# A hybrid encoder layer on one core: the order of weight pairs in the input chunks, six pairs in five output chunks, and some work moved by a step or more

## The chip, the core and the metric

The kernel runs on one core of a Trainium2 chip. Its engines are TensorE (PE; its weight loads are a row of their own, PEld), VectorE (DVE), ScalarE (ACT), GpSimd (POOL) and SyncE (SP, which issues nearly all DMAs). The metric is the time on the device in microseconds: 1500.56 us is the median of three runs (1500.46 to 1501.62).

## The reference

All in float32, with 256 tokens and a width of 4096. The factors that the matrices have are left out here.

```python
h = layer_norm(x, emb_ln_g, emb_ln_b)
p = h @ w_in                                  # 256 x 4096 @ 4096 x 13312: c_b, c_c, c_h, c_z, a_q, a_k, a_v, a_z
y_conv = c_b * conv3_centred(c_c * c_h, conv_w) * silu(c_z)
y_attn = banded_window_attention(a_q, a_k, a_v, sink) * silu(a_z)   # 16 heads of 128, 4 kv heads, window 128, ALiBi, sink
y = concatenate([y_conv, y_attn]) @ w_out     # 256 x 4096 @ 4096 x 4096
out = layer_norm(2 ** 0.25 * h + y, ln_g, ln_b)
```

## The kernel before

**Products.** Both projections are done in three products of a rounded type: each operand is split into a high half (rounded) and a low half (the rest), and hi x hi, lo x hi and hi x lo are summed. The activations lie in `xT`, transposed, hi and lo. The weights are streamed: each piece is loaded from memory as float32, ScalarE writes its high half (`split_hi`, tile `whi`, L226), VectorE subtracts for its low half (`split_lo`, tile `wlo`, L230), and TensorE reads both. There are three buffers of `whi` and three of `wlo`, so the splitting runs at most three steps ahead.

**Chunks and steps.** The input projection is cut into 26 chunks of 512 columns (two for k and v, then for each of four groups a gate z and a q, then for each of four groups cc, ch, cz, cb), the output projection into 9 (seven of 512 columns, two of 256). A chunk is a row of steps, written as a string. An "s" is a whole piece: 4 k-tiles by 512 columns, 1,024 KB, 48 matmuls of 256 columns. An "S" is a pair: 2 k-tiles, 512 KB, computed with seven block products in place of eight (a Strassen scheme), 21 matmuls. A pair needs sums of weight blocks (`sums`, on VectorE before the split) and sums of activation blocks, which are made once (`x_sums`, into `SC`; for the output projection `y_sums`, into `SCy`). Two pairs that follow each other are a couple: their sums are made in one go (L192 to L194 in place of L205 to L207 twice), and both must then lie in the four slots of the tile `wall`; a single pair or a piece can also be loaded into other places (`w6` to `w8`, or `R` in the output chunks).

**A step.** Step j does, in this order: the matmuls of step j, `split_hi(j + 3)`, whatever was booked for the step with `at`, the loads that have room (`loads`), `sums(j + 4)`, `split_lo(j + 3)`. Nothing else schedules: each engine works through its instructions in that order, SP through its DMAs, with semaphores between.

**Attention.** It runs beside the chunks, booked by `SPREAD`: after a q chunk each of the group's four heads gets a step for each of its parts: scores, s_add (L601), exps, recip, norms, p_tr (probabilities transposed, and their high half by ScalarE, L636), p_lo (their low half by VectorE, L641), pv (L648 and L650), out_z (L654, which also stores to `yd`). The transposes of z (L518) share a PSUM pool of two banks with them.

**Output chunks.** `residual` prepares alpha times the normed input from loaded rows (`gb`: two scale rows and ln_g; `xc`: x), `end_out` adds it and takes statistics, `end_out2` multiplies by ln_g. `rows_load` and `rows_split` prepare ln_g and ln_b as rows for the last norm: 15 small DMAs (L908).

Of the kernel before, what the change touches and what calls it, by code (L numbers as in the profile page):

```python
# [34 lines left out]
NPC = KT // PK  # L35
# [6 lines left out]
HT = S // 2  # L42
NP = 8
NP1 = 4
PAIRS = [0, 0, NP1] + [NP] * (len(IN_ORDER) - 3)
ORDERS = {0: "s" * 8, NP1: "sssSSsSsSs", NP: "sSSsSSSSsSSs"}
OUT = 100
OP = 4
OUT_ORDERS = ["s" * 8] * 2 + ["sSsSsSsSss"] * 5 + ["", ""]
N_W = 4  # L50
OFF = 4
GAP = 64
# [49 lines left out]
def encoder_kernel(ctx: ExitStack, tc: tile.TileContext, x, emb_g, emb_b, wi, ws, conv_w, sink, wo, ln_g, ln_b, out):  # L102
# [21 lines left out]
    def couple(j):  # L124
# [5 lines left out]
    psc = pw = pc = R = None  # L130
    extra = []
    user = {}
    in_R = [(steps.index(("opair", OUT + 4, OP - 1)) + 1, "R0"), (steps.index(("opair", OUT + 4, OP - 1)) + 1, "R1"),
            (steps.index(("opair", OUT + 6, OP - 1)) + 1, "R2")]

    def w_bufs(j):

# [520 lines left out]
    def head(n, *steps):  # L658
        return [(t, f, n) for t, f in zip(steps, (scores, s_add, exps, recip, norms, p_tr, p_lo, pv, out_z))]

    SPREAD = [(6, q_tr, 0), (7, q_lo, 0), (10, q_tr, 1), (11, q_lo, 1)] + head(0, 8, 9, 9, 10, 10, 13, 15, 19, 20) + head(
        1, 9, 10, 10, 11, 12, 19, 21, 22, 23) + head(2, 13, 17, 18, 19, 20, 24, 27, 28, 29) + head(
        3, 21, 22, 22, 23, 23, 28, 30, 31, 32)

    def open_pc():
        nonlocal pc
# [115 lines left out]
        for hi, lo, y in y_parts(q):  # L782
            nc.vector.tensor_tensor(lo, y, hi.bitcast(F32), op=ALU.subtract)

    X_SUMS = [NPC + 2 + k for k in range(NP1)] + [2 * NPC + k for k in (1, 4, 6, 8)]
    build_tab()
    later = {}

    def at(j, fn, *a):
        later.setdefault(j, []).append((fn, a))  # L790
# [76 lines left out]
    def bcast(src, a, n):  # L867
        return bass.AP(tensor=src.tensor, offset=src.offset + a, ap=[[0, P], [1, n]])
# [32 lines left out]
    def rows_split():  # L901
        for k, (slots_h, slot_l) in enumerate((((0, 1), 2), ((3,), 4))):
            w, hl = lnw[k], R[0:KT, k, 3 * W + P:3 * W + 3 * P].bitcast(F32R).rearrange("p (a b) -> p a b", a=2)
            nc.vector.tensor_copy(hl[:, 0, :], w)
            nc.vector.tensor_tensor(hl[:, 1, :], w, hl[:, 0, :].bitcast(F32), op=ALU.subtract)
            for b, a0, n in ((0, 0, 12), (32, 12, 12), (64, 24, 8)):
                for r, h in [(r, 0) for r in slots_h] + [(slot_l, 1)]:
                    nc.sync.dma_start(out=rows[b + r:b + r + 1, 0:n * P].bitcast(F32), in_=hl[a0:a0 + n, h, :].bitcast(F32))  # L908

    def res_load(n):  # L910
        if n >= ncs:
            return
        c0, w, _, _ = chunks[n]
        if n < ncs - 1:
            gb = p2.tile([P, 3, w], F32, name="gb")
        if n < ncs - 2:
            xc = p2.tile([P, 2, W], F32, name="xc")[:, :, 0:w]
        elif n == ncs - 2:
            xc = z_tile()[:, 6 * W:6 * W + 2 * w].rearrange("p (a b) -> p a b", a=2)
        else:  # L920
            z = zt[0]
            gb = z[:, 0:3 * w].rearrange("p (a b) -> p a b", a=3)
# [7 lines left out]
        nc.sync.dma_start(out=gb[:, 2, :], in_=bcast(ln_g, c0, w))  # L930
        for i in range(2):
            nc.sync.dma_start(out=xc[:, i, :], in_=x[i * P:(i + 1) * P, c0:c0 + w])
        res[n] = gb, xc

    def residual(n):
        gb, xc = res[n]
        for i in range(2):
            nc.vector.scalar_tensor_tensor(xc[:, i, :], xc[:, i, :], musd[:, i, 0:1], gb[:, 0, :],
                                           op0=ALU.subtract, op1=ALU.mult)
            nc.vector.scalar_tensor_tensor(xc[:, i, :], xc[:, i, :], musd[:, i, 2:3], gb[:, 1, :],  # L940
                                           op0=ALU.mult, op1=ALU.add)
# [34 lines left out]
        return r  # L976

    def end_out2(n, i, r):
        nc.vector.tensor_tensor(r, r, res[n][0][:, 2, :], op=ALU.mult)
# [189 lines left out]
```

## Time and profile before

| | |
|---|---|
| median of three runs | 1500.56 us |
| profiled execution | 1500.92 us, span 1499.2 us |
| granted TensorE clock, mean | 0.999 |
| TensorE busy | 1482.4 us (99%), 12,878 matmuls |
| VectorE, ScalarE busy | 1338.4 us (89%), 803.3 us (54%) |
| DMA | 316.17 MB, 211 GB/s over the span |
| per chunk of the input projection with eight pairs | 40.8 us (688.0 to 728.8) to 46.9 us (285.0 to 331.9) |
| per output chunk with four pairs | 42.1 to 42.2 us |

A row of a group reads: line, engine, operation, out<-in, shapes, count | busy us, mean ns of one | idle us of the engine before it and what ended that. A matmul's busy time overlaps the next one's, so what TensorE loses at a wait is read from the weight loads. A wait is put down to the engine whose signal the profile takes for the last.

### The profile page before, as it was taken

The numbers are of one execution on the slowest core, as the hardware profiler recorded it, in microseconds if no ns is written. First come the engines' busy times: TensorE is split into PE (matmuls) and PEld (weight loads), VectorE is DVE, ScalarE is ACT, GpSimd is POOL, SyncE is SP. The second block draws the span as 40 slices with busy tenths as digits, with TensorE's granted clock in tenths as the row PEclk, the third lists the DMA queues.
The fourth block names the chain that finished last, engine by engine and source line by source line (L and its number), as shares of the span: only waits on it lengthen the run. The fifth ranks groups of instructions, "written<-read, shape, count | busy, mean of one in ns | idle before, by whom it ended". The sixth has DMA issues, their size and how long they took to land.

```text
span 1499.2 us, 29810 instructions
## 1 busy us (share of the span) xinstructions
PE 1482.4 (99%) x12878; PEld 1465.4 (98%) x12878; DVE 1338.4 (89%) x1384; ACT 803.3 (54%) x687; POOL 1.3 (0%) x7
## 2 busy tenths in 40 slices
PE   7999999999999999999999999999999999999998
PEld 4999999999999999999999999999999999999997
DVE  7768999898999999999999999999998688888876
ACT  5544656766666665655555555555555444444431
POOL 0000000000000000000000000000000000000000
PEclk9999999999999999999999999999999999999999
DMA  8545465555554556646545655556558656756663
GB/s 318 217 183 196 164 217 189 192 197 208 180 204 176 190 201 209 230 177 224 200 182 219 231 198 197 225 204 241 191 207 313 233 201 220 290 215 230 219 237 113
DMA packets 71365, 316.17 MB, mean 211 GB/s; under 512 B 8545, under 2 KB 12609, under 8 KB 50113
## 3 DMA queue, kind: packets, MB, share of 16 engines
q1 hardware_dynamic: 70224, 312.43, 57.3%
q8 instruction: 101, 1.65, 0.4%
q10 hardware_dynamic: 1008, 1.84, 0.3%
q14 instruction: 32, 0.25, 0.0%
HBM read 305.23 MB, written 8.91 MB: 210 GB/s over the span
## 4 chain that ended last, share of the span: by engine, by line
PE 93%; DVE 3%; ACT 1%; issue 1%; DMA 1%; SPq 0%; ACTq 0%; DVEq 0%
PE acc L275 39%; PE acc L957 20%; PE pacc L301 6%; PE pacc L300 6%; PE pacc L303 6%; PE acc L301 4%; PE acc L300 4%; PE acc L303 4%; DVE wlo L230 1%; PE att L518 1%; ACT whi L226 1%; DVE st L354 0%; PE acc L404 0%; DMA wall<-in_ws 0%; DVE wall L192 0%
## 5 line engine op out<-in xcount | busy, mean ns | idle before, releaser
L226 ACT ACTIVATE whi<-wall 128x1792 fp32r<-128x1792 f32 (+1 forms) x284 | 501.7, 1772 | 464.6 <-DVE wall L194 149.7
L230 DVE TENSOR_TENSOR wlo<-wall,whi 128x1792 fp32r<-128x1792 f32 (+1 forms) x284 | 593.4, 2096 | 75.9 <-ACT whi L226 64.3
L275 PE MATMUL acc<-whi,xT 128*128 128x256 f32 x3584 | 427.6, 276 | 0.0
L275 PEld LDWEIGHTS acc<-whi,xT 128*128 128x128 f32 x3584 | 415.8, 188 | 0.0
L275 PE MATMUL acc<-wlo,xT 128*128 128x256 f32 x1792 | 221.3, 275 | 0.0
L275 PEld LDWEIGHTS acc<-wlo,xT 128*128 128x128 f32 x1792 | 211.4, 188 | 0.0
L226 ACT ACTIVATE whi<-w 128x2048 fp32r<-128x2048 f32 x73 | 140.7, 1927 | 114.6 <-PE acc L275 72.5
L957 PE MATMUL acc<-whi,xT 128*128 128x256 f32 x1696 | 201.8, 275 | 0.0
L957 PEld LDWEIGHTS acc<-whi,xT 128*128 128x128 f32 x1696 | 196.6, 188 | 0.4 <-issue 0.4
L230 DVE TENSOR_TENSOR wlo<-w,whi 128x2048 fp32r<-128x2048 f32 x73 | 166.8, 2286 | 10.8 <-ACT whi L226 10.6
L192 DVE TENSOR_TENSOR wall<-wall 128x1024 f32<-128x1024 f32 x93 | 113.3, 1218 | 11.0 <-DMA wall<-in_ws 8.7
L300 PE MATMUL acc<-whi,xT 128*128 128x256 f32 x416 | 114.7, 276 | 0.0
L301 PE MATMUL acc<-whi,xT 128*128 128x256 f32 x416 | 114.6, 276 | 0.0
L300 PE MATMUL pacc<-whi,xT 128*128 128x256 f32 x396 | 111.0, 280 | 0.0
L303 PE MATMUL pacc<-wlo,xT 128*128 128x256 f32 x396 | 109.2, 276 | 0.6 <-DVE wlo L230 0.4
L301 PE MATMUL pacc<-whi,xT 128*128 128x256 f32 x396 | 109.1, 276 | 0.0
L957 PE MATMUL acc<-wlo,xT 128*128 128x256 f32 x848 | 105.3, 275 | 0.0
L303 PE MATMUL acc<-wlo,xT 128*128 128x256 f32 x416 | 104.4, 275 | 0.0
L300 PE MATMUL pacc<-whi,SC 128*128 128x256 f32 x376 | 103.6, 275 | 0.0
L301 PE MATMUL pacc<-whi,SC 128*128 128x256 f32 x376 | 103.6, 275 | 0.0
L957 PEld LDWEIGHTS acc<-wlo,xT 128*128 128x128 f32 x848 | 100.4, 188 | 0.0
L303 PE MATMUL pacc<-wlo,SC 128*128 128x256 f32 x376 | 94.5, 276 | 0.0
(224 smaller groups left out, 1930.1 us busy)
## 6 DMA issues: line engine op xcount, KB each, us to landing
wall<-in_ws SPq DMA_DIRECT2D x202, 512.0 KB
w<-in_wi SPq DMA_DIRECT2D x73, 1024.0 KB
wall<-in_wo SPq DMA_DIRECT2D x43, 1024.0 KB
wall<-in_wi SPq DMA_DIRECT2D x39, 1024.0 KB
R<-in_wo SPq DMA_DIRECT2D x10, 1024.0 KB
x<-in_x SPq DMA_DIRECT2D x7, 512.0 KB
yl<-yd SPq DMA_DIRECT2D x7, 512.0 KB
xc<-in_x SPq DMA_DIRECT2D x14, 256.0 KB
```

What stands on the lines that cost most here:

```text
L192: nc.vector.tensor_tensor(t[:, :, 4:6, :], t[:, :, 1:3, :], t[:, :, 0:1, :].to_broadcast([P, 2, 2, HW]), op=ALU.add)
L226: nc.scalar.activation(part(j, wh[j]), part(j, raw[j]), AF.Copy)
L230: nc.vector.tensor_tensor(part(j, wl[j]), part(j, raw[j]), part(j, wh[j]).bitcast(F32), op=ALU.subtract)
L275: nc.tensor.matmul(acc[ci, i][:, c:c + HW], x, w[:, k * W + c:k * W + c + HW], start=(first and w is hi and k + off + c == 0), stop=(last ...
L300: nc.tensor.matmul(o, ah, hi[:, w, :], start=(opens and p == 0), stop=False)
L301: nc.tensor.matmul(o, al, hi[:, w, :], start=False, stop=False)
L303: nc.tensor.matmul(o, ah, lo[:, w, :], start=False, stop=(closes and last))
L518: nc.tensor.transpose(ps[:, c, i * P:(i + 1) * P], t[:, i, (2 * b + c) * P:(2 * b + c + 1) * P], ident)
L957: nc.tensor.matmul(acc[ci, i][:, c:c + HW], y, m[:, k * w + c:k * w + c + HW], start=(first and off + c == 0), stop=(last and c + HW == w))
```

## The change

- In the 23 input chunks with eight pairs the order goes from s SS s SSSS s SS s to s SSSS s SS s SS s.
- Output chunks 2 to 6 have six pairs and five pieces in place of four and six. The pairs stand in couples. Two more `y_sums` are made, and all six start three steps sooner, in output chunk 0.
- `p_lo` of the four heads stands one, one, two and one step sooner.
- The `x_sums` of pair 7 move from step 24, in the chunk before, to step 31, in the first chunk that needs them.
- ln_g gets a tile of its own with two buffers (`lg`), so `end_out2` can come three steps later; `residual` comes two steps later.
- `rows_load` and `rows_split` come a chunk sooner, and the 15 DMAs are booked two a step.

```diff
-ORDERS = {0: "s" * 8, NP1: "sssSSsSsSs", NP: "sSSsSSSSsSSs"}
+ORDERS = {0: "s" * 8, NP1: "sssSSsSsSs", NP: "sSSSSsSSsSSs"}
 OUT = 100
-OP = 4
-OUT_ORDERS = ["s" * 8] * 2 + ["sSsSsSsSss"] * 5 + ["", ""]
+OP = 6
+OUT_ORDERS = ["s" * 8] * 2 + ["sSSsSSsSSss"] * 5 + ["", ""]
...
-    SPREAD = [(6, q_tr, 0), (7, q_lo, 0), (10, q_tr, 1), (11, q_lo, 1)] + head(0, 8, 9, 9, 10, 10, 13, 15, 19, 20) + head(
-        1, 9, 10, 10, 11, 12, 19, 21, 22, 23) + head(2, 13, 17, 18, 19, 20, 24, 27, 28, 29) + head(
-        3, 21, 22, 22, 23, 23, 28, 30, 31, 32)
+    SPREAD = [(6, q_tr, 0), (7, q_lo, 0), (10, q_tr, 1), (11, q_lo, 1)] + head(0, 8, 9, 9, 10, 10, 13, 14, 19, 20) + head(
+        1, 9, 10, 10, 11, 12, 19, 20, 22, 23) + head(2, 13, 17, 18, 19, 20, 24, 25, 28, 29) + head(
+        3, 21, 22, 22, 23, 23, 28, 29, 31, 32)
...
-    X_SUMS = [NPC + 2 + k for k in range(NP1)] + [2 * NPC + k for k in (1, 4, 6, 8)]
+    X_SUMS = [NPC + 2 + k for k in range(NP1)] + [2 * NPC + k for k in (1, 4, 6, 15)]
...
-                    nc.sync.dma_start(out=rows[b + r:b + r + 1, 0:n * P].bitcast(F32), in_=hl[a0:a0 + n, h, :].bitcast(F32))
+                    row_moves.append((rows[b + r:b + r + 1, 0:n * P].bitcast(F32), hl[a0:a0 + n, h, :].bitcast(F32)))
+        for k, (o, i) in enumerate(row_moves):
+            at(j + 1 + k // 2, row_move, o, i)
...
-            gb = p2.tile([P, 3, w], F32, name="gb")
+            gb = p2.tile([P, 2, w], F32, name="gb")
+            lg = p2.tile([P, w], F32, name="lg", bufs=2)
...
     for k in range(OP):
-        at(chunks[1][3] + 1 + k, y_sums, k)
+        at(N_IN + 6 + k, y_sums, k)
...
-            if t == 0 and n:
+            if t == (3 if n < ncs - 2 else 0) and n:
                 for a in ends:
                     end_out2(*a)
                 ends = []
-                if n < ncs - 1:
-                    res_load(n)
-            if t == (0 if n == ncs - 1 else 2 if n == ncs - 2 else 4 if n else 7):
+            if t == 0 and 0 < n < ncs - 1:
+                res_load(n)
+            if t == (0 if n == ncs - 1 else 2 if n == ncs - 2 else 6 if n else 7):
                 residual(n)
-            if n == 2 and t == 4:
+            if n == 1 and t == 4:
                 rows_load()
-            if n == 2 and t == 8:
-                rows_split()
+            if n == 1 and t == 6:
+                rows_split(j)
```

Three places show what it does to the order.

VectorE, around the low half of the probabilities of a group's fourth head (`kp` is the tile that holds the probabilities, `wlo` the low halves of weights, `wall` rows are the sums of a couple, `zT` is `out_z` of the head before). Before:

```order
L230 TENSOR_TENSOR wlo0_3425<-wall_92,whi_3409 128x1792
L654 TENSOR_TENSOR zT_2019<-att_3411,zT_2019 128x256
L192 TENSOR_TENSOR wall_92<-wall_92 128x2x512
L193 TENSOR_TENSOR wall_92<-wall_92 128x2x256
L194 TENSOR_TENSOR wall_92<-wall_92 128x2x256
L230 TENSOR_TENSOR wlo1_3456<-w6_3299,whi_3448 128x2048
L641 TENSOR_TENSOR kp_645<-att_3418,kp_645 128x512
L230 TENSOR_TENSOR wlo2_3489<-wall_92,whi_3479 128x1792
```

After:

```order
L230 TENSOR_TENSOR wlo0_3399<-wall_92,whi_3381 128x1792
L654 TENSOR_TENSOR zT_2021<-att_3383,zT_2021 128x256
L641 TENSOR_TENSOR kp_645<-att_3390,kp_645 128x512
L192 TENSOR_TENSOR wall_92<-wall_92 128x2x512
L193 TENSOR_TENSOR wall_92<-wall_92 128x2x256
L194 TENSOR_TENSOR wall_92<-wall_92 128x2x256
L230 TENSOR_TENSOR wlo1_3458<-wall_92,whi_3449 128x2048
L230 TENSOR_TENSOR wlo2_3491<-wall_92,whi_3481 128x1792
```

The low half (L641) has moved ahead of a couple's sums and of the split of a whole piece.

SP, at the end of a q chunk in attention (`in_ws` is a pair's load, `in_wi` a piece's, `yd` the store of `out_z`, `kp<-kd` the reload of k). Before:

```order
L172 DMA wall_92<-in_ws 128x1024 x2
L172 DMA wall_92<-in_wi 128x2048 x2
L172 DMA wall_92<-in_ws 128x1024
L655 DMA yd0_72<-zT_2019 128x256
L172 DMA wall_92<-in_ws 128x1024
L172 DMA w6_3042<-in_wi 128x2048
L172 DMA wall_92<-in_ws 128x1024
L554 DMA kp_645<-kd_648 128x512
```

After:

```order
L172 DMA wall_92<-in_ws 128x1024 x2
L172 DMA w6_2848<-in_wi 128x2048
L172 DMA wall_92<-in_wi 128x2048
L172 DMA wall_92<-in_ws 128x1024 x2
L655 DMA yd0_72<-zT_2021 128x256
L172 DMA wall_92<-in_ws 128x1024
L554 DMA kp_645<-kd_648 128x512
```

Both loads of the next chunk's first couple now stand ahead of the store, and one of the two pieces goes to `w6` in place of `wall`.

VectorE, in the middle of an output chunk with pairs (L938 and L940, after L945 and L947, are `residual`; L205 to L207 are the sums of one pair, L192 to L194 those of a couple). Before:

```order
L230 TENSOR_TENSOR wlo0_15077<-wall_92,whi_15074 128x1792
L938 SCALAR_TENSOR_TENSOR xc_14907<-xc_14907,musd_87,gb_14906 128x512
L940 SCALAR_TENSOR_TENSOR xc_14907<-xc_14907,musd_87,gb_14906 128x512
L938 SCALAR_TENSOR_TENSOR xc_14907<-xc_14907,musd_87,gb_14906 128x512
L940 SCALAR_TENSOR_TENSOR xc_14907<-xc_14907,musd_87,gb_14906 128x512
L230 TENSOR_TENSOR wlo1_15107<-wall_92,whi_15104 128x2048
L230 TENSOR_TENSOR wlo2_15160<-wall_92,whi_15157 128x2048
L205 TENSOR_TENSOR R_13290<-R_13290 128x512
L206 TENSOR_TENSOR R_13290<-R_13290 128x256
L207 TENSOR_TENSOR R_13290<-R_13290 128x256
L230 TENSOR_TENSOR wlo0_15190<-wall_92,whi_15183 128x2048
```

After:

```order
L230 TENSOR_TENSOR wlo0_15084<-wall_92,whi_15081 128x1792
L230 TENSOR_TENSOR wlo1_15137<-R_13290,whi_15134 128x2048
L945 SCALAR_TENSOR_TENSOR xc_14916<-xc_14916,musd_87,gb_14914 128x512
L947 SCALAR_TENSOR_TENSOR xc_14916<-xc_14916,musd_87,gb_14914 128x512
L945 SCALAR_TENSOR_TENSOR xc_14916<-xc_14916,musd_87,gb_14914 128x512
L947 SCALAR_TENSOR_TENSOR xc_14916<-xc_14916,musd_87,gb_14914 128x512
L230 TENSOR_TENSOR wlo2_15167<-wall_92,whi_15164 128x2048
L192 TENSOR_TENSOR wall_92<-wall_92 128x2x512
L193 TENSOR_TENSOR wall_92<-wall_92 128x2x256
L194 TENSOR_TENSOR wall_92<-wall_92 128x2x256
L230 TENSOR_TENSOR wlo0_15197<-wall_92,whi_15190 128x2048
```

The residual stands a split later, and behind it the sums are those of a couple, in `wall`, in place of one pair's in `R`.

More of the change, by code (lines that the diff above doesn't have):

```diff
@@ L132, in encoder_kernel @@
     user = {}
-    in_R = [(steps.index(("opair", OUT + 4, OP - 1)) + 1, "R0"), (steps.index(("opair", OUT + 4, OP - 1)) + 1, "R1"),
-            (steps.index(("opair", OUT + 6, OP - 1)) + 1, "R2")]
+    in_R = [(steps.index(("opair", OUT + 4, npairs(OUT + 4) - 1)) + 1, "R0"), (steps.index(("opair", OUT + 4, npairs(OUT + 4) - 1)) + 1, "R1"),
+            (steps.index(("opair", OUT + 6, npairs(OUT + 6) - 1)) + 1, "R2")]
     def w_bufs(j):
@@ L888, in encoder_kernel @@
     lnw = {}
-    first_cols, zt = [], []
+    first_cols, zt, row_moves = [], [], []
     def z_tile():
@@ L899, in rows_load, with rows_split @@
             nc.sync.dma_start(out=w, in_=src.rearrange("(a b) -> a b", b=P))
-    def rows_split():
+    def rows_split(j):
         for k, (slots_h, slot_l) in enumerate((((0, 1), 2), ((3,), 4))):
@@ L907, in rows_split, with row_move @@
                 for r, h in [(r, 0) for r in slots_h] + [(slot_l, 1)]:
-                    nc.sync.dma_start(out=rows[b + r:b + r + 1, 0:n * P].bitcast(F32), in_=hl[a0:a0 + n, h, :].bitcast(F32))
+                    row_moves.append((rows[b + r:b + r + 1, 0:n * P].bitcast(F32), hl[a0:a0 + n, h, :].bitcast(F32)))
+        for k, (o, i) in enumerate(row_moves):
+            at(j + 1 + k // 2, row_move, o, i)
+    def row_move(o, i):
+        nc.sync.dma_start(out=o, in_=i)
     def res_load(n):
@@ L921, in res_load @@
             z = zt[0]
-            gb = z[:, 0:3 * w].rearrange("p (a b) -> p a b", a=3)
+            gb = z[:, 0:2 * w].rearrange("p (a b) -> p a b", a=2)
+            lg = z[:, 2 * w:3 * w]
             xc = z[:, 3 * w:5 * w].rearrange("p (a b) -> p a b", a=2)
@@ L929, in res_load @@
         nc.sync.dma_start(out=gb[:, 1, :], in_=bcast(emb_br, c0, w))
-        nc.sync.dma_start(out=gb[:, 2, :], in_=bcast(ln_g, c0, w))
+        nc.sync.dma_start(out=lg, in_=bcast(ln_g, c0, w))
         for i in range(2):
             nc.sync.dma_start(out=xc[:, i, :], in_=x[i * P:(i + 1) * P, c0:c0 + w])
-        res[n] = gb, xc
+        res[n] = gb, xc, lg
     def residual(n):
-        gb, xc = res[n]
+        gb, xc, _ = res[n]
         for i in range(2):
@@ L978, in end_out2 @@
     def end_out2(n, i, r):
-        nc.vector.tensor_tensor(r, r, res[n][0][:, 2, :], op=ALU.mult)
+        nc.vector.tensor_tensor(r, r, res[n][2], op=ALU.mult)
     def finish_lhs(n, i):
@@ L1038, in y_sums @@
         if k == 0:
-            t = p2.tile([P, 6, 2, 4, HT], F32R, name="SCy", tag="SC")
+            t = p2.tile([P, OP, 2, 4, HT], F32R, name="SCy", tag="SC")
             SC = [t[:, p, :, :, :] for p in range(OP)]
```

## The prediction

> **What bounds the kernel now.** I read the page's head and busy part first, then the chain that ended last, then what TensorE waited for, then stretches of the span chunk by chunk.
>
> ```profile
> span 1499.2 us, 29810 instructions
> ...
> PE 1482.4 (99%) x12878; PEld 1465.4 (98%) x12878; DVE 1338.4 (89%) x1384; ACT 803.3 (54%) x687; POOL 1.3 (0%) x7
> ...
> PE 93%; DVE 3%; ACT 1%; issue 1%; DMA 1%; SPq 0%; ACTq 0%; DVEq 0%
> ```
>
> TensorE is busy 99% of the span and carries 93% of the chain that ended last. So a change can gain in two ways only: fewer matmuls, or fewer places where TensorE stands. The profiled execution took 1500.9 us (span 1499.2 and 1.7 around it); the median of the three runs is 1500.56, 0.36 less. I sum against the execution and take off 0.36 at the end. About 0.2% (3.0 us) is what a measurement of this kernel can tell from no change.
>
> Where TensorE stands is best read from its weight loads (PEld), since a matmul's row goes on for 0.28 us while the next starts 0.11 after it. Of the waits by engine and releaser (us in total, times, longest):
>
> ```profile
> PEld att L417 <- issue: 9.4, 3, 8.3
> ...
> PEld att L648 <- ACT qhl L576: 2.1, 3, 0.8
> ...
> PEld att L518 <- DVE m L601: 1.1, 2, 0.8
> ...
> PEld pacc L303 <- DVE wlo L230: 1.0, 2, 0.6
> ...
> PEld att L650 <- DVE kp L641: 0.3, 1, 0.3
> ```
>
> The 9.4 us are the start, before the input has come, which the change leaves alone. The other four are stalls in the middle, 4.5 us in eight places. By stretches (us, then each engine's busy time and instructions, granted clock, DMA share, GB/s), a convolution chunk of the input projection, output chunks 0 and 1, and output chunk 4:
>
> ```profile
> 646.20:688.00 41.80, 41.80 (x370) 41.80 (x369) 41.09 (x34) 22.59 (x14) 0.00 (x0) 1.00 0.60 214
> 1141.70:1186.20 44.50, 44.50 (x394) 44.50 (x394) 29.03 (x22) 20.26 (x15) 0.00 (x0) 1.00 0.73 261
> 1186.20:1229.70 43.50, 43.50 (x386) 43.50 (x385) 38.88 (x52) 17.68 (x13) 0.00 (x0) 1.00 0.62 229
> 1314.00:1356.20 42.20, 42.20 (x374) 42.20 (x374) 36.96 (x38) 18.93 (x12) 0.00 (x0) 1.00 0.56 200
> ```
>
> In an output chunk TensorE never stands: 42.20 us for 374 matmuls, 0.113 us each at full clock (1.00). VectorE has 36.96 of 42.20. In the convolution chunk VectorE is at 41.09 of 41.80 and TensorE still does not stand; I lean on that row below.
>
> **The change part by part.** Durations (busy, mean ns of one) are these:
>
> ```profile
> L230 DVE TENSOR_TENSOR wlo<-wall,whi 128x1792 fp32r<-128x1792 f32 x202 | 406.4, 2018 | 30.2 <-ACT whi L226 18.7 <-PE acc L957 11.4
> L230 DVE TENSOR_TENSOR wlo<-wall,whi 128x2048 fp32r<-128x2048 f32 x82 | 187.6, 2288 | 45.7 <-ACT whi L226 45.6
> L192 DVE TENSOR_TENSOR wall<-wall 128x1024 f32<-128x1024 f32 x93 | 113.3, 1218 | 11.0 <-DMA wall<-in_ws 8.7 <-issue 2.2
> L193 DVE TENSOR_TENSOR wall<-wall 128x512 f32<-128x512 f32 x93 | 64.4, 692 | 3.2
> L205 DVE TENSOR_TENSOR wall<-wall 128x512 f32<-128x512 f32 x16 | 10.9, 684 | 1.6 <-DMA wall<-in_ws 1.6
> L207 DVE TENSOR_TENSOR wall<-wall 128x256 f32<-128x256 f32 x16 | 6.8, 425 | 0.6
> ...
> L226 ACT ACTIVATE whi<-wall 128x1792 fp32r<-128x1792 f32 x202 | 343.7, 1709 | 309.5 <-DVE wall L194 149.7 <-PE pacc L301 61.6 <-PE acc L275 39.3
> L226 ACT ACTIVATE whi<-wall 128x2048 fp32r<-128x2048 f32 x82 | 158.0, 1927 | 155.2 <-PE acc L957 65.4 <-PE pacc L301 33.2 <-PE acc L275 31.8
> ...
> L636 ACT ACTIVATE kp<-att 128x512 fp32r<-128x512 f32 x16 | 9.4, 586 | 1.6 <-PE att L634 1.6
> ```
>
> *Six pairs in five output chunks.* A whole piece is 48 matmuls (4 k-tiles x 2 x 2 x 3), a pair 21 (7 products x 3). A chunk goes from 6 x 48 + 4 x 21 = 372 to 5 x 48 + 6 x 21 = 366. Five chunks lose 30 matmuls; at 0.113 us that is 3.4 us, straight off the engine that bounds: **-3.4**. The Trainium skill (TensorE: Matmul & The Clock Gate, Back-to-back issue gap) gives sustained spacings of 81 ns at 128 columns and 131 at 512; a line between them makes an estimate of 98 ns for 256, and 2.9 us for the 30. The trace disagrees with 113, which decides.
>
> VectorE pays for it. Splitting: 6 x 2.02 + 5 x 2.29 against 4 x 2.02 + 6 x 2.29, +1.8 a chunk. Sums: three couples of 1.22 + 0.69 + 0.69 (L194 costs what L193 does) against four single pairs of 0.68 + 0.43 + 0.43, +1.6. That lifts 36.96 to 40.4 in a chunk that shrinks to 41.5: 97%. The cover is what is left of the chunk, 1.1 us, and a lead of up to three split pieces. The convolution chunk runs at 98% with no stall, so I take 0 at this place; if the cover goes, up to 1 us a chunk, so bounds 0 to +5. ScalarE: 2 x 1.71 - 1.93 = +1.5 us a chunk, on 18.93 of 42.20: nothing. The two extra y_sums cost VectorE what an x_sums does (3.4 us each, worked out below); two of the six now stand in output chunk 0, where it has 29.03 of 44.50 busy, the other four in chunk 1 as before: nothing, and if that cover were gone, 7 us.
>
> *p_lo sooner.* All four stalls at L648 and L650 are the fourth head of a group (p_lo at step 30, pv at 31). One of them, VectorE, then ScalarE, then the weight loads (start, duration):
>
> ```profile
> 310.62 2.29 DVE L230 TENSOR_TENSOR wlo<-w,whi 128x2048 fp32r<-128x2048 f32 x1
> 312.83 0.68 DVE L641 TENSOR_TENSOR kp<-att,kp 128x512 fp32r<-128x512 f32 x1
> ...
> 312.49 0.59 ACT L576 ACTIVATE qhl<-att 128x512 fp32r<-128x512 f32 x1
> ...
> 313.62 0.53 PEld L648 LDWEIGHTS att<-kp,v 128*128 128x128 f32 x4 [0.69 <-ACT qhl L576]
> ```
>
> The wait is written down to L576, but that ended at 313.08; p_lo (L641) ended at 313.51 and the loads started 0.11 later. p_lo stands behind sums and a 2.29 us split. One step sooner it stands ahead of both, some 5 us earlier, against a lateness of 0.7. I take all of 2.1 + 0.3: **-2.4**; bounds -2.4 to 0. What it can cost: p_lo waits for ScalarE's copy of the same head (L636, 0.59), issued a step before; if that is late, the sums and the split queued behind p_lo on VectorE wait up to 0.6 us more, which TensorE sees only where the lead is smaller. I take 0.
>
> *Loads in a new order.* The stalls at L518 come from late loads. One of them:
>
> ```profile
> 371.46 1.22 DVE L192 TENSOR_TENSOR wall<-wall 128x1024 f32<-128x1024 f32 x1 [2.22 <-issue]
> ...
> 374.06 2.28 DVE L230 TENSOR_TENSOR wlo<-wall,whi 128x2048 fp32r<-128x2048 f32 x1
> ...
> 376.26 0.47 DVE L601 CUSTOM_DVE_ANT_0 s<-th,att,sk 128x256 f32<-128x256 f32 x1
> ...
> 377.19 0.42 PEld L518 LDWEIGHTS att<-ident,z 128*128 128x128 f32 x4 [0.77 <-DVE m L601]
> ```
>
> VectorE stood 2.22 us before the sums of the next chunk's first couple, so s_add (L601) came late and held the transposes. In SP's queue the second load of that couple stood behind the move yd<-zT, which waits for VectorE; now both stand ahead of it. The 2.22 covers the 0.77. I take **-1.1**; bounds -1.1 to 0.
>
> *Four pairs at a chunk's front, and the last x_sums.* Eight pairs and four pieces stay eight and four, so nothing is added per chunk. "s" and four pairs cost VectorE 2.29 + 4 x 2.02 + 2 x 2.60 = 15.6 us against 102 + 30 = 132 matmuls, 14.9 us, of TensorE: 0.7 short. Before, that run stood in the middle of the chunk, behind one piece; now the previous chunk's last piece stands ahead of the first, and 5.4 - 2.3 = 3.1 us of lead come with it. That is better cover than before: 0. In the first such chunk the old place shows:
>
> ```profile
> 171.44 2.02 DVE L230 TENSOR_TENSOR wlo<-wall,whi 128x1792 fp32r<-128x1792 f32 x1
> 173.37 1.28 DVE L717 TENSOR_TENSOR z<-acc,z 128x512 f32<-128x512 f32 x2
> 174.57 3.95 DVE L230 TENSOR_TENSOR wlo<-wall,whi 128x1792 fp32r<-128x1792 f32 x2
> ...
> 173.51 0.19 PEld L303 LDWEIGHTS pacc<-wlo,xT 128*128 128x128 f32 x1 [0.33 <-DVE wlo L230]
> ```
>
> Here the end of the previous chunk (L717) lies inside the run. Now the run is over when L717 comes: **-1.0**. But the x_sums of pair 7 go into this chunk, behind the run:
>
> ```profile
> L675 DVE TENSOR_TENSOR xs<-xT 128x512 f32<-128x512 f32 x8 | 5.5, 683 | 0.0
> L523 DVE TENSOR_TENSOR SC<-xs,SC 128x384 fp32r<-128x384 f32 x8 | 4.5, 558 | 6.7 <-ACT SC L522 6.7
> L680 DVE TENSOR_TENSOR xs<-xs 128x128 f32<-128x128 f32 x32 | 7.9, 287 | 0.5
> ```
>
> 0.68 + 1.0 + 0.56 + 0.28 with 0.8 of waiting for ScalarE (6.7 over 8) is 3.4 us. From the run's fourth split to the split of the chunk's third piece VectorE then has 2.0 + 2.6 + 2.3 + 1.3 + 4.0 + 3.4 + 2.6 + 2.3 = 20.5, less 0.08 of overlap per instruction about 19.8, behind a split of 1.7 on ScalarE that starts when the run's first pair is through its whi products. TensorE in that time has 0.8 (that pair's wlo products) + 3 x 2.4 + 5.4 + 2 x 2.4 + 3.6 = 21.8. 21.5 against 21.8, with the signals between engines not counted, is even: a new stall of 0 to 1.5, I take **+0.4**.
>
> *Row moves and what else is moved.* The moves hold SP for 11.50 us, with the weight loads behind them (the first row); the other two are residual and end_out2 on VectorE:
>
> ```profile
> 1270.23 11.50 SPq L908 DMA_DIRECT2D rows<-R  x15
> ...
> L940 DVE SCALAR_TENSOR_TENSOR xc<-xc,musd,gb 128x512 f32<-128x512 f32 x14 | 10.5, 752 | 0.5
> L979 DVE TENSOR_TENSOR R<-R,gb 128x512 f32<-128x512 f32 x14 | 9.0, 684 | 0.0
> ```
>
> No stall of TensorE follows it in the row of chunk 4 or in the waits, so spreading them gains nothing: 0. end_out2 three steps later, residual two later and ln_g in a tile of its own move 4 x 0.75 and 2 x 0.68 us of VectorE inside a chunk, ahead of plus_res: 0.
>
> Sum: -3.4 - 2.4 - 1.1 - 1.0 + 0.4 = -7.5. 1500.9 - 7.5 = 1493.4, against the median **1493.1 us**.
>
> **The rivals.** *Half of it:* the 30 matmuls go, but VectorE's lateness comes back at other places of the same chunks, with 4.5 us as before. For it speaks that VectorE is at 98% in the input chunks. 1500.56 - 3.4 = 1497.2.
> *Output chunks run late:* VectorE at 97%, and couples that need two of the four wall slots at once, so loads come later. At 1 us a chunk, 7.5 - 5 = 2.5 are left: 1498.1, within 0.2%. Against it: 3.1 us of lead behind each run, and DMA at 0.56. The Trainium skill (DMA: Bandwidth & Descriptors, Rules for kernel authors) asks for 1 MiB or more per transfer, and its section Bandwidth has 341 GB/s for 1 MB and 138 for 64 KB; one piece of 1,024 KB becomes two of 512, which halfway (an estimate of 240 GB/s) takes 1.3 us more a chunk, 6.5 in all, and 1499.6 if nothing hid it. The trace disagrees: 261 GB/s at a share of 0.73 where no pairs are loaded and 214 at 0.60 where most loads are 512 KB are both 357 per full share.
> *Slower:* the four pairs at the front eat the lead in all 23 chunks that have them. If VectorE enters the run with none, each is short by the 0.7 worked out above: 23 x 0.7 = 16 - 7.5 = +8.6, so 1509. It decides from 0.33 us a chunk on. Against it is the 3.1 us of the piece ahead.
>
> **How the numbers follow.** Forecast 0.66, with a range of its own from 1491.7 (every stall gone, no new one, and a microsecond of small ones) to 1495. Half of it 0.17; output chunks late 0.10; slower 0.07. The range 1491.2 to 1497.9 takes in the forecast and half of it. Half of it lies just past 0.2%: 0.15 of its 0.17 count as faster, so faster 0.81, same 0.12, slower 0.07.
>
> **What would show it.** 12,848 matmuls instead of 12,878; output chunks 2 to 6 of 41.5 us with TensorE busy throughout and VectorE near 40.4; no wait at L648, L650 or L518 for z; at most one at about 180 us for wlo. Wrong it would be if TensorE waits for wlo or whi in several input chunks, for wlo in the output chunks, or if VectorE there waits for wall<-in_ws.

## The result, and the profile after

| | before | after |
|---|---|---|
| median | 1500.95 us (1500.46 to 1501.62, 4 runs) | 1492.56 us (1492.42 to 1493.00, 4 runs) |
| span of the profiled execution | 1499.2 us | 1490.7 us |
| ratio | | 0.9946, 95% interval 0.9934 to 0.9957 |

The forecast was 1493.1. The page's head and busy part of after, and the chain that ended last:

```profile
span 1490.7 us, 29750 instructions
...
PE 1477.3 (99%) x12848; PEld 1461.6 (98%) x12848; DVE 1358.1 (91%) x1386; ACT 806.9 (54%) x694; POOL 1.3 (0%) x7
...
PE 98%; DVE 1%; ACT 0%; DMA 0%; issue 0%; SPq 0%; DVEq 0%; ACTq 0%
```

There are 30 matmuls fewer, as forecast, and TensorE now carries 98% of the chain in place of 93%. VectorE got 19.7 us more work and the span is 8.5 us shorter: its work was on the path only where it was late. The weight loads' waits after (us in total, times, longest):

```profile
PEld att L417 <- issue: 9.7, 3, 8.6
...
PEld acc L275 <- DVE wlo L230: 0.4, 1, 0.4
```

The first row is the start, as before. Of the rows at L648, L518, L303 and L650 none is left; the second row is the one new wait, at 183 us. Stretches of after (us, each engine's busy time and instructions, granted clock, DMA share, GB/s): the first z chunk, which has four pairs; the chunk behind it, the first with eight; a convolution chunk; output chunk 4:

```profile
111.74:153.90 42.16, 42.16 (x374) 42.16 (x373) 37.09 (x47) 21.83 (x22) 0.00 (x0) 1.00 0.49 167
153.90:196.19 42.29, 42.10 (x370) 41.90 (x369) 40.46 (x40) 25.25 (x20) 0.00 (x0) 1.00 0.53 195
641.95:683.75 41.80, 41.80 (x370) 41.80 (x369) 41.04 (x35) 22.05 (x14) 0.00 (x0) 1.00 0.60 213
1308.20:1349.68 41.48, 41.48 (x368) 41.48 (x367) 39.68 (x37) 20.07 (x13) 0.00 (x0) 1.00 0.66 230
```

The output chunk takes 41.48 us as forecast, with VectorE at 39.68 (forecast 40.4). Only the second row has TensorE short of its stretch.

Below, a chunk's time is from its first matmul to the next chunk's. Summed over places, in the profiled executions, against before, with experiments 1, 2, 3 and 5 beside it:

| us against before | first chunk with eight pairs (154 to 196 us) | next nine, with attention beside them (to 601) | convolution (to 1137) | output chunks 2 to 6 | median |
|---|---|---|---|---|---|
| after | -0.69 | -4.08 | 0.00 | -3.40 | -8.4 |
| 1: output part alone | +0.09 | -0.10 | -0.14 | -3.40 | -2.6 |
| 2: order of the pairs alone | -0.71 | +3.54 | -0.14 | 0.00 | +2.4 |
| 3: p_lo alone | +0.08 | -2.20 | -0.14 | 0.00 | -2.7 |
| 5: order and p_lo together | -0.69 | -4.08 | 0.00 | 0.00 | -3.9 |

The 0.14 are some 0.02 in every second convolution chunk, with no wait, and stay unexplained. The chunks are those of one execution and the medians are of several: beside the chunks a median has the start and the end of an execution, and waits that come and go between executions (experiment 6). From the issue of the last store to the span's end, with the same instructions, it is 3.4 to 3.8 us in the four profiles with the output part of before, 3.1 to 3.2 in those with that of after, but 4.4 in experiment 1, which has it too. What sets it stays open.

### The profile page after: what moved, and what is told of

Read it like the earlier page. It is cut to its first block, busy times and chain, and to the rows that moved or that the text cites. A ratio compares the mean times of both kernels' runs of the same rounds, so it can differ in the third digit from the quotient of the medians.

```text
span 1490.7 us, 29750 instructions
## 1 busy us (share of the span) xinstructions
PE 1477.3 (99%) x12848; PEld 1461.6 (98%) x12848; DVE 1358.1 (91%) x1386; ACT 806.9 (54%) x694; POOL 1.3 (0%) x7
## 4 chain that ended last, share of the span: by engine, by line
PE 98%; DVE 1%; ACT 0%; DMA 0%; issue 0%; SPq 0%; DVEq 0%; ACTq 0%
PE acc L275 41%; PE acc L964 18%; PE pacc L301 7%; PE pacc L303 7%; PE pacc L300 7%; PE acc L301 5%; PE acc L300 5%; PE acc L303 5%; PE att L518 1%; DVE st L354 0%; PE att L648 0%; PE att L634 0%; PE acc L404 0%; DMA x<-in_x 0%; PE att L387 0%; DVE x L362 0%
## 5 line engine op out<-in xcount | busy, mean ns | idle before, releaser
L275 PEld LDWEIGHTS acc<-whi,xT 128*128 128x128 f32 x3584 | 415.8, 188 | 0.0
L275 PE MATMUL acc<-wlo,xT 128*128 128x256 f32 x1792 | 221.4, 275 | 0.2 <-DVE wlo L230 0.2
L275 PEld LDWEIGHTS acc<-wlo,xT 128*128 128x128 f32 x1792 | 211.5, 188 | 0.4 <-DVE wlo L230 0.4
L964 PEld LDWEIGHTS acc<-whi,xT 128*128 128x128 f32 x1536 | 178.1, 188 | 0.4 <-issue 0.4
L192 DVE TENSOR_TENSOR wall<-wall 128x1024 f32<-128x1024 f32 x108 | 131.5, 1218 | 10.9 <-DMA wall<-in_ws 8.1
L300 PE MATMUL pacc<-whi,xT 128*128 128x256 f32 x406 | 113.3, 279 | 0.0
L301 PE MATMUL pacc<-whi,xT 128*128 128x256 f32 x406 | 111.8, 275 | 0.0
L303 PE MATMUL pacc<-wlo,xT 128*128 128x256 f32 x406 | 111.7, 275 | 0.0
L303 PE MATMUL acc<-wlo,xT 128*128 128x256 f32 x436 | 109.4, 275 | 0.0
L964 PE MATMUL acc<-wlo,xT 128*128 128x256 f32 x768 | 95.5, 275 | 0.0
L303 PE MATMUL pacc<-wlo,SC 128*128 128x256 f32 x376 | 94.5, 275 | 0.0
L964 PEld LDWEIGHTS acc<-wlo,xT 128*128 128x128 f32 x768 | 90.9, 188 | 0.0
```

The source lines that it names most:

```text
L192: nc.vector.tensor_tensor(t[:, :, 4:6, :], t[:, :, 1:3, :], t[:, :, 0:1, :].to_broadcast([P, 2, 2, HW]), op=ALU.add)
L275: nc.tensor.matmul(acc[ci, i][:, c:c + HW], x, w[:, k * W + c:k * W + c + HW], start=(first and w is hi and k + off + c == 0), stop=(last ...
L300: nc.tensor.matmul(o, ah, hi[:, w, :], start=(opens and p == 0), stop=False)
L301: nc.tensor.matmul(o, al, hi[:, w, :], start=False, stop=False)
L303: nc.tensor.matmul(o, ah, lo[:, w, :], start=False, stop=(closes and last))
L964: nc.tensor.matmul(acc[ci, i][:, c:c + HW], y, m[:, k * w + c:k * w + c + HW], start=(first and off + c == 0), stop=(last and c + HW == w))
```

## The experiments

**1. The output part alone.** The changed kernel with these edits undone:

```diff
-ORDERS = {0: "s" * 8, NP1: "sssSSsSsSs", NP: "sSSSSsSSsSSs"}
+ORDERS = {0: "s" * 8, NP1: "sssSSsSsSs", NP: "sSSsSSSSsSSs"}
-... head(0, ..., 13, 14, ...) + head(1, ..., 19, 20, ...) + head(2, ..., 24, 25, ...) + head(3, ..., 28, 29, ...)
+... head(0, ..., 13, 15, ...) + head(1, ..., 19, 21, ...) + head(2, ..., 24, 27, ...) + head(3, ..., 28, 30, ...)
-    X_SUMS = ... (1, 4, 6, 15)]
+    X_SUMS = ... (1, 4, 6, 8)]
```

> The input part is that of the kernel before (order of the pairs, place of p_lo, x_sums of pair 7); the output part is that of the changed kernel (six pairs in five chunks, y_sums, residual, end_out2, row moves). If the terms of the prediction add up, this gives the -3.4 alone: 1500.95 - 3.4 = 1497.5, 12,848 matmuls, output chunks 2 to 6 of 41.5 us without a wait of TensorE, and in the input part the 4.5 us of waits at L648, L518, L303 and L650 as before. If instead the output chunks owe part of their good result to the input part, a wait for wlo or whi shows in them and the time is 1498 or more.

1498.39 us (1497.49 to 1499.0, 11 runs) against 1501.02; ratio 0.9982, 0.9973 to 0.999. The five chunks lost 0.68 each, with no wait, and the waits of the input part stand as before:

```profile
PEld att L648 <- ACT qhl L576: 2.3, 3, 0.8
...
PEld att L518 <- DVE m L601: 1.1, 3, 0.4
PEld pacc L303 <- DVE wlo L230: 1.1, 2, 0.6
```

So the output chunks owe nothing to the input part.

**2 and 3. The order alone, p_lo alone.** The kernel before with the first edit below (2), and with the second (3):

```diff
-ORDERS = {..., NP: "sSSsSSSSsSSs"}
+ORDERS = {..., NP: "sSSSSsSSsSSs"}
-    X_SUMS = ... (1, 4, 6, 8)]
+    X_SUMS = ... (1, 4, 6, 15)]
```
```diff
-... head(0, ..., 13, 15, ...) + head(1, ..., 19, 21, ...) + head(2, ..., 24, 27, ...) + head(3, ..., 28, 30, ...)
+... head(0, ..., 13, 14, ...) + head(1, ..., 19, 20, ...) + head(2, ..., 24, 25, ...) + head(3, ..., 28, 29, ...)
```

> The kernel before with the new order of the pairs in the input chunks and the x_sums of pair 7 at its new step, nothing else. If the waits at L518 come from loads that stand behind the store of out_z in SP's queue, and the one at L303 from the old place of the run, they go: -1.1 - 1.0, with a new wait of 0.4 near 183 us: 1500.95 - 1.7 = 1499.2, and the waits at L648 and L650 stay at about 2.4. Rival: the waits at L518 are part of the same lateness of VectorE as those at L648; then they stay, and the gain is 0.6 or less.

> The kernel before with p_lo of the four heads at its new steps, nothing else. If p_lo was late only because it stood behind sums and a split, the waits at L648 and L650 go, those at L518 (1.1) and L303 (1.0) stay: 1500.95 - 2.4 = 1498.5. Rival (half of it): the 0.7 us that VectorE spends on p_lo sooner makes the sums and splits behind it late, and the waits at L518 grow by what those at L648 lose: 1499.7 or more.

The order alone is **slower**: 1503.40 us (1502.84 to 1505.82, 11 runs), ratio 1.0017, 1.0008 to 1.0026. Both theories missed that. Its waits:

```profile
PEld att L650 <- DVE kp L641: 3.2, 5, 1.1
PEld att L648 <- ACT qhl L576: 3.0, 3, 1.9
...
PEld att L592 <- DVE zT L654: 0.7, 1, 0.7
...
PEld acc L275 <- DVE wlo L230: 0.4, 1, 0.4
```

L518 and L303 are gone, as the working said; but where before had 2.1 at L648 and 0.3 at L650 there are now 6.2. Two of these waits, VectorE and then the weight loads (start, duration):

```profile
382.63 6.00 DVE L230 TENSOR_TENSOR wlo<-wall,whi 128x1792 fp32r<-128x1792 f32 x3
...
391.14 2.29 DVE L230 TENSOR_TENSOR wlo<-w,whi 128x2048 fp32r<-128x2048 f32 x1
393.34 0.69 DVE L641 TENSOR_TENSOR kp<-att,kp 128x512 fp32r<-128x512 f32 x1
...
401.81 1.23 DVE L192 TENSOR_TENSOR wall<-wall 128x1024 f32<-128x1024 f32 x1 [2.38 <-DMA wall<-in_ws]
...
406.61 0.68 DVE L641 TENSOR_TENSOR kp<-att,kp 128x512 fp32r<-128x512 f32 x1
...
394.08 0.30 PEld L650 LDWEIGHTS att<-kp,v 128*128 128x128 f32 x2 [0.58 <-DVE kp L641]
407.40 0.53 PEld L648 LDWEIGHTS att<-kp,v 128*128 128x128 f32 x4 [1.86 <-ACT qhl L576]
```

At 393 us p_lo (L641) stands behind three splits, a couple's sums and one more split: the run of four pairs now ends where p_lo of the third head is booked. At 406 it stands behind a couple's sums that had waited 2.38 us for their load, and behind a split.

p_lo alone: 1498.29 us (1497.3 to 1499.03, 11 runs), ratio 0.9982, 0.9973 to 0.9991. L648 and L650 are gone, and the waits for z, 1.1 before, are 1.9:

```profile
PEld att L518 <- DVE m L601: 1.9, 3, 1.2
...
PEld pacc L303 <- DVE wlo L230: 1.1, 2, 0.6
```

So its own theory held, and a small part of the rival's: 0.8 of the 2.4 came back at L518.

**5. Both together.** The kernel before with the edits of 2 and 3.

> The kernel before with all three edits of the input part (order of the pairs, place of p_lo, x_sums of pair 7), the output part as before. The order alone cost 2.4 us, because with p_lo at its old steps its wait moved to L650 and grew (3.0 at L648 and 3.2 at L650); p_lo alone gained 2.7. If the two need each other, together they give what the chunks of the changed kernel show: -4.5 to -4.8, no wait at L648, L650, L518 or L592, one of 0.35 near 183 us: 1501.0 - 4.6 = 1496.4. If the two parts simply add up, +2.4 - 2.7 = -0.3: 1500.7.

1496.89 us (1495.97 to 1497.48, 8 runs) against 1500.76, ratio 0.9973, 0.9962 to 0.9983. Chunk by chunk it is the input part of the changed kernel, -4.77 in the first two columns of the table. The two alone sum to +0.71 there. The edits need each other: p_lo sooner is what keeps the new order from costing, and the new order takes the waits at L518 that p_lo left.

**4. The row moves as before.** The changed kernel with the rows loaded, split and moved where the kernel before does it:

```diff
-            at(j + 1 + k // 2, row_move, o, i)
+            row_move(o, i)
-            if n == 1 and t == 4:
+            if n == 2 and t == 4:
                 rows_load()
-            if n == 1 and t == 6:
+            if n == 2 and t == 8:
```

> The changed kernel with the rows of the last norm loaded and moved where the kernel before does it: all 15 moves at once, in output chunk 2. The prediction costs the spreading at 0, since no wait of TensorE followed the 11.5 us that the moves hold SP: then 1492.6. Rival: with six pairs in couples, both loads of a couple need a slot of wall at the same time and have less room to be late, so the 11.5 us on SP now reach TensorE: a wait for wlo or whi in output chunk 2 or 3 of 3 to 7 us, 1495.6 to 1499.6. Then the spreading is what makes six pairs free, though by itself it gains nothing.

1498.36 us (1497.36 to 1499.84, 10 runs), ratio to before 0.9982, 0.9973 to 0.9991: 4.9 to 5.8 more than the two sets of runs of the changed kernel (1492.56, and 1493.47 in experiment 6). The rival had it. SP, VectorE, the weight loads, and stretches of that place:

```profile
1264.91 11.62 SPq L913 DMA_DIRECT2D rows<-R  x15
1276.63 0.38 SPq L172 DMA_DIRECT2D wall<-in_ws  x1
...
1279.91 1.22 DVE L192 TENSOR_TENSOR wall<-wall 128x1024 f32<-128x1024 f32 x1 [4.84 <-DMA wall<-in_ws]
...
1284.84 2.23 PEld L964 LDWEIGHTS acc<-wlo,xT 128*128 128x128 f32 x16 [3.19 <-DVE wlo L230]
...
1284.70:1286.70 2.00, 1.86 (x14) 1.86 (x15) 2.00 (x3) 2.00 (x2) 0.00 (x0) 0.91 0.59 206
1286.70:1289.70 3.00, 3.00 (x16) 3.00 (x15) 1.96 (x2) 1.14 (x1) 0.00 (x0) 0.50 1.08 419
1289.70:1291.70 2.00, 2.00 (x19) 2.00 (x18) 0.41 (x1) 0.00 (x0) 0.00 (x0) 0.98 1.00 416
```

Read it downwards: the moves hold SP for 11.62 us; the load behind them is issued at 1276.63; VectorE stands 4.84 us for it; TensorE stands 3.19 us for the split. Then the granted clock is 0.50; in the 3 us shown of it 16 matmuls run where 26 would. The chunk is 4.95 longer. In the kernel before, with four single pairs a chunk, 11.50 us of moves on SP cost TensorE nothing. This run undoes two edits at once, the chunk in which the moves stand and their spreading over steps, and no run tells which of the two is needed; nor was it run apart whether the couples or the two additional pairs use up the room.

**6. The changed kernel again.**

> The changed kernel once more, unchanged, beside the others of this call: 1492.6. Its start was 0.3 longer and its end 0.6 shorter than in the profile of before, which no edit explains; if these are the scatter of single executions, they come out otherwise here.

1493.47 us (1492.76 to 1493.88, 5 runs), ratio 0.9949, 0.9937 to 0.9962. The end came out as in the first profile, so the 0.6 there is no scatter of one execution. The start is: over all profiles, of whatever kernel, the transposes of the input's second half (L369) begin between 21.8 and 22.4 us, and the second chunk between 66.9 and 67.5. And there is a wait that the first profile lacks. The same sums in the first profile, then in this one, and the weight loads in this one:

```profile
353.26 1.23 DVE L192 TENSOR_TENSOR wall<-wall 128x1024 f32<-128x1024 f32 x1 [0.46 <-DMA wall<-in_ws]
```
```profile
355.04 1.23 DVE L192 TENSOR_TENSOR wall<-wall 128x1024 f32<-128x1024 f32 x1 [2.19 <-DMA wall<-in_ws]
...
366.24 0.19 PEld L592 LDWEIGHTS att<-kp,qhl 128*128 128x128 f32 x1 [0.59 <-DVE zT L654]
```

Their load was issued at 349.89 and at 349.93; the sums could start 3.4 us later in one execution and 5.1 in the other, and out_z (L654) came behind by as much. The profiles of experiments 4, 8, 10 and 12 have this wait too, those of 5, 7 and 9 do not: the changed kernel stands on an edge there, worth 0.7 us.

**8 and 12. The x_sums of pair 7**, at step 33 (8) and back at step 24 (12), in place of 31:

```diff
-    X_SUMS = ... (1, 4, 6, 15)]
+    X_SUMS = ... (1, 4, 6, 17)]      # 8
+    X_SUMS = ... (1, 4, 6, 8)]       # 12
```

> The changed kernel with the x_sums of pair 7 at step 33 in place of 31. The prediction put a new wait of 0.4 behind x_sums (3.4 us of VectorE ahead of a split); the trace has 0.35 + 0.11 at 183 us. If the x_sums are its cause, two steps later it goes: chunk of 41.8 in place of 42.3 us, 1492.1. If it is the length of the run itself (15.6 us of VectorE against 14.9 of TensorE) it stays: 1492.6.

> The changed kernel with the x_sums of pair 7 back at step 24, in the chunk before. Then they take 3.4 us of VectorE just ahead of the first run of four pairs: a wait for wlo in that run near 165 us of 0.5 to 1.5, and the one at 183 goes or stays small: 1492.6 to 1493.5. If the place of x_sums does not matter, the one wait of 0.46 at 183 us stays as it is: 1492.6.

8: 1492.35 us (1492.09 to 1492.96, 5 runs); the wait is gone and the chunk 0.51 shorter, so x_sums were its cause. 12: 1494.69 us (1494.22 to 1495.49, 4 runs), that chunk 2.36 longer than in after, and not for the reason expected. The run itself lost only 0.3; VectorE and the weight loads of 12:

```profile
180.66 1.23 DVE L192 TENSOR_TENSOR wall<-wall 128x1024 f32<-128x1024 f32 x1 [3.16 <-DMA wall<-in_ws]
...
185.59 1.92 PEld L275 LDWEIGHTS acc<-wlo,xT 128*128 128x128 f32 x16 [2.35 <-DVE wlo L230]
```

x_sums ahead of the run push its splits back by 2.5 us. The slots of `wall` come free as much later (the second load of the third couple is out at 175.9 us, in after at 173.3), and VectorE stands 3.16 us for it. In experiment 8 that wait is 1.46 us; at step 31 x_sums lie in it, and are done 1.6 us after the load.

**9 and 10. How much room the output chunks have.** Two and six more VectorE operations in each of the five chunks:

```diff
+            if 2 <= n < ncs - 2 and t == 7:
+                for _ in range(2):                # 10: range(6)
+                    nc.vector.tensor_tensor(res[n][2], res[n][2], res[n][2], op=ALU.max)
```

> The changed kernel with two additional VectorE operations of 128x512 (0.69 us each) in each of the output chunks 2 to 6; they write back what they read. VectorE has 39.68 of 41.48 us there, so 1.8 are left: 41.05 of 41.48, no wait of TensorE, 1492.6. Rival (output chunks run late): the four-step window of a run of pairs has no room and the 1.4 us come out in each chunk: 5 x 1.4 = 6.9, 1499.5.

> The same with six additional operations a chunk, 4.1 us: VectorE would need 43.8 in 41.5. Short by 2.3 a chunk, 11.6 over five chunks. If the lead of the splitting covers the first 3 to 5 us, the time is 1492.6 + 6.6 to 8.6 = 1499.2 to 1501.2, with the waits for wlo in the later chunks; if the lead does not carry over from chunk to chunk, all 11.6 show, 1504.

9: 1493.13 us (1492.95 to 1493.52, 4 runs), as the changed kernel; one wait of 0.3, in the fifth chunk. 10: 1506.15 us (1505.21 to 1506.62, 6 runs), ratio to before 1.0033, 1.0022 to 1.0045. Its waits, and stretches of the third and the fourth of the five chunks:

```profile
PEld acc L964 <- DVE wlo L230: 8.9, 4, 2.5
...
1312.60:1355.80 43.20, 41.80 (x368) 41.61 (x367) 42.58 (x42) 19.17 (x12) 0.00 (x0) 1.00 0.68 226
1355.80:1401.70 45.90, 43.66 (x368) 43.34 (x367) 43.92 (x43) 19.69 (x12) 0.00 (x0) 0.96 0.63 212
```

The first chunk pays nothing (its 2.3 come out of the lead), the other four lose 4.09, 1.70, 4.41 and 2.61, 12.8 in all: more than either end of what was expected. The waits are near the working, 8.9 against 11.6 - 2.3 = 9.3, so the lead is worth some 2.7 us (11.6 - 8.9), once in the five chunks. Most of the other 4 us are the clock, 0.96 in one row: behind two of the four waits it falls to 0.50, which no theory had.

**11. Six pairs at the front** of the 23 chunks:

```diff
-ORDERS = {..., NP: "sSSSSsSSsSSs"}
+ORDERS = {..., NP: "sSSSSSSsSSss"}
```

> The changed kernel with the order s SSSSSS s SS s s in the 23 input chunks with eight pairs: the run at the front is six pairs in place of four. The working of the prediction: s and four pairs are 0.7 us short on VectorE against 3.1 us of lead; s and six pairs take VectorE 2.29 + 6 x 2.02 + 3 x 2.60 = 22.2 against 174 matmuls, 19.7: 2.5 short, still under 3.1. So no wait where VectorE does nothing else in the run, and about 1 us in the 8 attention chunks, where the chunk's end and s_add lie in it: 1492.6 + 4 to 8. Rival (the front eats the lead): the lead is worth 1 us or less, each of 23 runs comes short by 1.5 or more: 1492.6 + 35 = 1527.

1514.16 us (1512.34 to 1516.44, 4 runs), ratio to before 1.0086, 1.0069 to 1.0103: some 21 over the changed kernel, between the two theories. Its waits, and SP, VectorE and TensorE in one convolution chunk:

```profile
PEld pacc L303 <- DVE wlo L230: 7.9, 12, 2.1
PEld att L592 <- DVE zT L654: 5.1, 3, 1.7
...
PEld att L518 <- DVE zT L654: 4.1, 3, 1.4
...
644.85 19.87 SPq L172 DMA_DIRECT2D wall<-in_ws  x4
...
667.69 1.23 DVE L192 TENSOR_TENSOR wall<-wall 128x1024 f32<-128x1024 f32 x1 [1.31 <-DMA wall<-in_ws]
...
672.35 0.19 PEld L303 LDWEIGHTS pacc<-wlo,xT 128*128 128x128 f32 x1 [1.45 <-DVE wlo L230]
```

VectorE stood 1.31 us for the third couple's load, and TensorE 1.45 for its split. SP spent 19.87 us on four loads of pairs, where one takes 0.33 to issue: a run of three couples needs six slots of `wall` and has four, which the working with durations alone left out. Of the 23 chunks 14 lost time, by 0.25 to 4.25 us. The 4.25 are the first of them, where the granted clock falls to 0.50 behind a wait of 2.11 us (last section). The L592 and L518 rows are out_z behind the longer run.

**7. A version that beats both**: six pairs in the first z chunk.

```diff
-NP1 = 4
-ORDERS = {0: "s" * 8, NP1: "sssSSsSsSs", NP: "sSSSSsSSsSSs"}
+NP1 = 6
+ORDERS = {0: "s" * 8, NP1: "ssSSsSSsSSs", NP: "sSSSSsSSsSSs"}
-    X_SUMS = [NPC + 2 + k for k in range(NP1)] + [2 * NPC + k for k in (1, 4, 6, 15)]
+    X_SUMS = [NPC + 2 + k for k in range(NP1)] + [2 * NPC + k for k in (4, 18)]
```

> A further version: the changed kernel with six pairs in place of four in the third chunk of the input projection, x_sums of six pairs in the chunk of v, where VectorE has 30.6 of 44.4 us busy, and those of pairs 6 and 7 at steps 20 and 34. 6 matmuls fewer, -0.68, and the wait of 0.46 at 183 us goes since x_sums of pair 7 stand behind the next split: 1492.6 - 1.1 = 1491.5. Rival: in the third chunk VectorE (37.1 of 42.2 us) gets a couple more, +2.6 + 1.75, and loses two x_sums, 6.8, but the first two couples come while v is still being finished: a wait of 1 to 2 us there, 1492 to 1493.5.

1491.40 us (1491.31 to 1491.58, 5 runs), ratio to before 0.9936, 0.9924 to 0.9949, against 1493.47 for the changed kernel beside it. The two chunks:

```profile
111.90:153.38 41.48, 41.48 (x368) 41.48 (x367) 37.94 (x42) 22.65 (x21) 0.00 (x0) 1.00 0.52 183
153.38:195.16 41.78, 41.78 (x370) 41.78 (x369) 37.79 (x35) 24.55 (x19) 0.00 (x0) 1.00 0.49 185
```

42.16 became 41.48, six matmuls at 0.113, and 42.29 became 41.78: the wait at 183 is gone. Of the 2.07 between the medians these two chunks make 1.2; another 0.7 is the wait at L592, which the profile of experiment 6 has and this one lacks. Between 40 us and the last chunk TensorE waits nowhere in this profile.

## Why the prediction was right, step by step

*Matmuls, -3.4:* -0.68 in each of five chunks, -3.40, with 113.3 ns a matmul in both kernels. The Trainium skill (TensorE: Matmul & The Clock Gate, Back-to-back issue gap) would by the estimate between its columns have 2.9. Experiment 7 agrees with the trace again: 0.68 for six, where 98 ns would give 0.59.

*VectorE in the output chunks, 0:* held. 39.68, not 40.4: the working took four pairs' splits out of the chunk of before, but that chunk has three of 2.02 and seven of 2.29 us, as one pair's split there covers 2,048 columns (0.3 us); and it added durations, where consecutive operations overlap by some 0.08 us, at 21 places after against 18 before (another 0.3). The room is 1.8 us a chunk: 1.4 more cost nothing that can be measured, 4.1 more cost 13. The rival that the output chunks run late did not come true, but the row moves decide that: see below.

*p_lo, -2.4, and the loads and the run, -1.1 and -1.0:* the waits went, and with the new wait they were to sum to -4.1, against -4.77 measured in the chunks. The step that failed, though the sum did not show it, is that these were worked out one by one, each against the trace of before. Alone, the order makes the nine chunks 3.5 us longer, where -1.1 was forecast, since the run of four falls on p_lo's old steps; the prediction asked what a run does to the splits and not what it does to p_lo, queued on the same engine. p_lo alone has 0.8 more at L518. Only the pair is worth what was forecast.

*The new wait behind x_sums, +0.4 (0 to 1.5):* 0.46 at 183 us (0.35 and 0.11 in the start times of two matmuls), by the mechanism named, as experiment 8 shows. That x_sums left at step 24 would have cost 2.4 more than this (experiment 12) was not seen.

*Row moves, 0:* right for the time of the changed kernel, but the reason was incomplete. That no stall followed the moves in the trace of before says nothing of the chunks after, where couples must both lie in `wall` before their sums start. Spreading the moves and having them a chunk sooner is worth 5 us there (4.95 in one chunk). Without it the forecast of 0 for the output chunks would have failed; that the change had it was luck as far as the prediction goes, which saw no gain in it.

*What else is moved, 0:* output chunks 0 and 1, with the earlier y_sums, are as long as before. The later residual and end_out2 and the tile for ln_g were not undone in any run: no wait in the output chunks agrees with 0, but whether six pairs need these moves stays open.

*Four pairs at the front, 0:* held in 23 chunks; the rival (slower) did not come. Its point is near, though: with two pairs more 14 chunks lose time, and in the one shown it is the slots of `wall` that run out, not the lead.

*Not forecast:* the start, +0.29, and the end, -0.62, in the profiled executions; the wait of 0.7 at L592 that some executions of the changed kernel have.

The sum: -3.40 - 4.77 + 0.29 - 0.62 = -8.50, the difference of the spans; the forecast was -7.5 against the profiled execution.

## What to carry to other kernels

Where engines work through fixed rows, an edit's price is that of the rows it now shares with its neighbours: work out a move together with the other moves of the change, on the new order, and ask of every small instruction behind a moved run who waits for it. An edit that gains nothing by the trace of before (here 15 small DMAs, spread out and a chunk sooner) can be what pays for another one. A run of loads can run out of buffer slots before it runs out of the engine's time, as in experiment 11: count both.

## What the runs showed of the hardware

Within the chunks, TensorE's granted clock fell to 0.50 for 3.4 us behind waits of 3.15 us (experiment 4), 2.34 and 2.40 us (10) and 2.11 us (11), a wait being what lies between the starts of two matmuls beyond the usual 0.113. It stayed at 1.00 behind waits of 2.42 (10), 2.32 (12) and 1.85 us (2) and all shorter ones. Where it falls, the wait costs 1.7 us more than itself, half of the 3.4.

What parts them is where a wait falls. In these traces the granted clock changes only at whole multiples of 3.413 us from where its record starts: at 372, 373, 398 and 399 of them in experiment 10, at 373 and 374 in 4, at 46 and 47 in 11. Below are such stretches, each with the one behind it, and the number after a stretch's length is how long TensorE was busy in it. They hold, in this order, the waits of 2.34 and 2.42 us (experiment 10), of 2.11 (11) and of 1.85 (2).

```profile
1280.87:1284.28 3.41, 1.23 (x11) 1.03 (x10) 3.41 (x3) 2.79 (x2) 0.00 (x0) 1.00 0.75 294
1284.28:1287.70 3.42, 3.42 (x19) 3.42 (x18) 3.42 (x3) 2.29 (x2) 0.00 (x0) 0.50 0.90 299
1413.99:1417.41 3.42, 2.09 (x19) 1.89 (x17) 3.35 (x4) 1.16 (x1) 0.00 (x0) 1.00 0.70 222
1417.41:1420.82 3.41, 2.49 (x21) 2.49 (x22) 3.41 (x3) 3.41 (x3) 0.00 (x0) 1.00 0.62 239
...
167.66:171.07 3.41, 1.46 (x13) 1.26 (x12) 3.41 (x3) 3.01 (x2) 0.00 (x0) 1.00 0.12 24
171.07:174.49 3.42, 3.42 (x19) 3.42 (x18) 3.42 (x4) 2.09 (x2) 0.00 (x0) 0.50 0.83 262
...
405.71:409.12 3.41, 1.72 (x15) 1.72 (x15) 3.41 (x3) 2.73 (x3) 0.00 (x0) 1.00 0.76 275
409.12:412.54 3.42, 3.42 (x33) 3.42 (x31) 2.97 (x4) 0.48 (x1) 0.00 (x0) 1.00 0.56 202
```

In the chunks of all the profiles the four stretches with TensorE busy for 1.17 to 1.52 us were followed by one at 0.50, and those with 1.72 or more were not: the wait of 2.42 us was split between two stretches and that of 2.34 lay within one. So the edge lies near half a stretch; how sharp it is stays open (behind the last chunk, in experiment 4, one with 1.82 was followed by 0.50). This is read from the traces afterwards, and no run was made to test it.

The Trainium skill (TensorE: Matmul & The Clock Gate, What's actually happening) has the clock halved after an idle window of about 3.4 us that runs freely. The stretches of 3.413 us agree with such a window; that 1.9 to 2.4 us of standing in one were enough does not agree with an idle window, and the measurement decides.

And one load, issued at the same time of the program to within 0.04 us, let its reader start after 3.4 us in one execution and 5.1 in another. In this kernel, slack of less than 1.7 us in front of a load does not hold in every execution.
